# Eleven shifted columns renewed by VectorE alone, and HGRN2's levels on gathered keys and queries, in a two-layer hybrid decoder step

## The chip, the cores and the metric

The kernel runs on one core of one Trainium2 chip. The metric is the device time of one execution, in microseconds (us), taken as the median of several runs. The engines are called as in the profile: PE is TensorE (matrix products), PEld its weight load, DVE is VectorE, ACT is ScalarE, POOL is GpSimd, and SP issues the transfers.

## The reference, cut to what matters

One inference step of a two-layer trunk over a prompt of 256 tokens and 8 samples of 4 tokens each, so 288 token columns, all in fp32. The model has 2048 features.

```python
for l in range(DEPTH):                       # DEPTH = 2
    if l % 2 == 0:                           # retention (4 heads) beside RG-LRU (8 blocks)
        mix = _even_mixer(x, ...)            # x @ w_in (2048 x 6144), ..., @ w_out
    else:                                    # HGRN2: 16 heads, state 128 x 128
        mix = _odd_mixer(x, ...)             # x @ w_in (2048 x 8192), ..., @ w_out
    x = _layer_norm(DN_ALPHA * x + mix, g, b)
    f = _conv_ffn(x, ...)                    # u, v = split(x @ w_up); (gelu(conv(u)) * v) @ w_down
    x = _layer_norm(DN_ALPHA * x + f, g, b)
# HGRN2 (_gla): S_t = diag(f_t) S_{t-1} + k_t v_t^T ;  o_t = S_t^T q_t
# _layer_norm: (x - mean) * rsqrt(var + eps) * g + b
```

All states after the prompt and after the samples are outputs too.

## The kernel before, in words

**Layout.** Features lie on the 128 partitions and the 288 tokens along the free dimension; `x[k]`, k = 0 to 15, is one row of 128 features. Every fp32 operand of a projection is split into a high part in the matrix engine's fp32r format and a low part that is the rest (`xh`, `xl` for x; `wh`, `wl` for weights). A projection is a list of output columns m of 128 features each. `gemm` (L383) computes a group of columns: for each tile (k, m) three products, `wh` with `xh`, `wh` with `xl`, `wl` with `xh`, summed into one PSUM bank of the pool `pm` (four banks). The other four banks are the pool `px`, which the mixers' small products and the sums of the norms use through `psx`. A group of four columns runs k by k over the first 12 rows, then column by column over the last four (`order`, L125).

**Weights.** They come in 1 MB pieces of 16 tiles on SP's queue. ACT copies half a piece (eight tiles) to `wh` (L342), and DVE subtracts to get `wl` (L352), some three halves ahead of use.

**Order.** PE, ACT, DVE and POOL run their instructions in the order in which the program writes them. Side work is written as generators in `Tasks`: `gemm` calls `tasks.tick()` after each tile (three products), a tick counts down all tasks and lets at most one of those that are due take a step, and a task's `yield n` asks for its next step n ticks later.

**Change of stage.** A layer norm needs all of x, but the next projection begins before it is done. Its first columns run on *shifted* operands: x minus a pivot, times the gain, split into `xh` and `xl` (`raw_step`, L571). Two more operand columns hold the gain's and the bias's part, so these products are 290 wide. `close` (L535) sums x and its squares through PE (`lns`, `lnq`, from `laccd` and `laccq`, which POOL adds up) and makes the mean `mu` and `rs`, the reciprocal deviation. `fold` (L648) then puts them into each finished shifted column in PSUM with two DVE operations (L652, L653), after which ACT takes the column out (L405) and its bank is free. Meanwhile `renorm` renews x itself (`ren_step`, L599): it subtracts `mu` (L605, POOL), multiplies by `rs` (L608, POOL and DVE by turns), and applies gain and bias (L612, ACT), one step every REN ticks; and `operands` splits the renewed x into `xh` and `xl` (`op_step`, L626; the low part in L415, POOL and DVE by turns), which may overwrite a row only when the last shifted group has read it (`freed`). `first_groups` (L725) writes this order; `groups_odd_in` and `groups_up` list the groups. There are three such changes: from the even mixer to the first feed-forward part (at 481 us), from there to the odd mixer (at 1325), and from the odd mixer to the second feed-forward part (at 1965). Seven columns are shifted: the output gates of heads 0 to 6, or the v columns of the feed-forward part. They are kept until their head or their u column comes.

**HGRN2's levels.** A head's prompt is treated in two chunks of 128 by doubling block lengths L = 1, 2, ..., 64 (`levels`, L1265). At each level keys of one half of every block meet queries of the other half in one product (`scores`, L1241), and DVE merges the result into the score matrix `AA` under a mask (`keep`, L1250). Then keys and queries are multiplied by the totals of the forget gate, and the totals are joined in pairs (`T`). The product's keys are first copied into one piece, E, by ACT (`gather`, L1235); its queries are read from `qc` in place, with a stride. A level of before stands so in the code:

```python
self.scores(i)                       # product of E and qc
# DVE: k *= totals; sample part of k (L <= 2); T
yield GAP_A                          # 2 ticks
# DVE: qc *= totals; sample part of qc (L <= 2)
self.keep(i)                         # DVE: merge the product into AA
self.gather(i + 1)                   # ACT: E of the next level
yield GAP_B + slow                   # 2 ticks, 3 for heads 0 and 1
```

Heads with three columns (forget f, query q, value v) follow one another every 48 ticks; from head 7 on the head's gate column makes it 64.

**Fourfold copies.** In the retention heads of the even mixer the 32 sample columns of k and v are copied four times side by side on POOL (`v4` in L836, `k4` in L1001), 16 copies of 128x32 per head, so that one transposition (`pst`) spreads them over the partitions.

Of the kernel before, what the change touches and what calls it, by code (L numbers as in the profile page):

```python
# [18 lines left out]
P = 128  # L19
# [28 lines left out]
G0 = 0  # L48
# [7 lines left out]
REN = 4  # L56
LAG = 4
AHEAD = 7
LOG = range(1, 17, 2)
MUG = range(0, 17, 2)  # L60
# [16 lines left out]

def groups_odd_in():
    out = [[48, 49, 50, 51], [52], [53, 54]]
    for h in range(H_HG - 2):  # L80
        out += [[16 + h], [h], [32 + h]] + [[48 + h]] * (h >= AHEAD)
    a, b = H_HG - 2, H_HG - 1
    out += [[16 + a], [a], [16 + b], [b], [32 + a], [48 + a], [32 + b], [48 + b]]
    return [("od_in", list(range(KT)), g) for g in out]
# [6 lines left out]
def groups_up(l, q):  # L91
    ms = [m for f in range(q * FQ, (q + 1) * FQ) for m in (f, FT + f)]
    if q == 0:
        v = ms[1:2 * AHEAD:2]
        out = [v[:4], v[4:5], v[5:]] + [[m] for m in ms[0:2 * AHEAD:2] + ms[2 * AHEAD:]]
    else:
        out = [[m] for m in ms]
    return [(f"up{l}", UP_K[l], g) for g in out]
# [154 lines left out]
def build(tc, A, phases="ACDF"):  # L253
# [11 lines left out]
    with contextlib.ExitStack() as est:  # L265
# [117 lines left out]
        def gemm(mat, ks, ms, rh, rl, need=None, done=None, post=None, w=T):  # L383
            ps = {m: pm.tile([P, 512], F32, tag="pm", name=f"ps_{mat}_{m}_{ks[0]}") for m in ms}
# [29 lines left out]
        def split_lo(k, src, eng=None):  # L414
            (eng or V).tensor_tensor(xl[k], src, xh[k].bitcast(F32), op=ALU.subtract)  # L415
# [36 lines left out]
        class Norm:  # L452
# [82 lines left out]
            def close(self):  # L535
                self.stat(KT - 1)
                yield 9
# [61 lines left out]
            def ren_step(self):  # L599
# [3 lines left out]
                if i < KT:  # L603
                    k = self.order[i]
                    G.tensor_tensor(x[k], x[k], self.mu, op=ALU.subtract)  # L605
                if 0 < i <= KT:
                    k = self.order[i - 1]
                    (G if i in MUG else V).tensor_tensor(x[k], x[k], self.rs, op=ALU.mult)  # L608
# [17 lines left out]
            def op_step(self):  # L626
# [5 lines left out]
                if i > 0:  # L632
                    split_lo(self.order[i - 1], x[self.order[i - 1]], G if i in LOG else V)

            def operands(self):
                while self.no <= KT:
                    if self.op_ready():
                        self.op_step()
                    yield 1
# [85 lines left out]
        def first_groups(mat, prev, gs, done, post=None):  # L725

            gs = iter(gs)
            if isinstance(prev, Norm):
                fold = prev.fold(done)
                gemm(mat, prev.order, next(gs), xhf, xlf, prev.need_raw, fold, w=T + 2)  # L730
                gemm(mat, prev.order, next(gs), xhf, xlf, None, fold, w=T + 2)
                tasks.spawn(prev.operands(), 1)
                gemm(mat, prev.order, next(gs), xhf, xlf, None, fold, prev.freed.add, T + 2)
# [36 lines left out]
        def even_in(eo, ea, o_rg, o_rt, prev, norm):  # L770
# [56 lines left out]
            def vals(h):  # L827
# [4 lines left out]
                def vdone(m, ps):  # L832
                    i = m - 16 - 2 * h
                    S.activation(vt[i], ps[:, :T], AF.Copy)
                    for r in range(4):
                        G.tensor_copy(v44[:, i, r, :], vt[i][:, TP:T])  # L836
# [158 lines left out]
        def ret_inner(rt, h, cv, kk, qq, hd):  # L995
# [3 lines left out]
            for kt in range(2):  # L999
                for r in range(4):  # L1000
                    G.tensor_copy(k44[:, kt, r, :], kk[kt][:, TP:T])  # L1001
# [173 lines left out]
        class HG:  # L1175
# [59 lines left out]
            def gather(self, i):  # L1235

                self.e = self.od.tile([P, P], F32, name=f"E{i}_{self.h}", tag="E", bufs=3)
                cut = lambda a: a.rearrange("p (n c l) -> p n c l", c=2, l=1 << i)
                S.activation(cut(self.e), early_half(self.k, 1 << i), AF.Copy)

            def scores(self, i):  # L1241
# [3 lines left out]
                mm(ps[:, :P], self.e, late_half(self.qc, L, True))  # L1245
# [19 lines left out]
            def levels(self):  # L1265
                h, tl, k, qc = self.h, self.tl, self.k, self.qc
                slow = 1 if h < 2 else 0
# [6 lines left out]
                for i in range(7):  # L1274
                    L = 1 << i
                    self.scores(i)
                    early, late = early_half(k, L), late_half(qc, L, False)
                    V.tensor_tensor(early, early, totals(cur, L, True), op=ALU.mult)
                    W = T if L <= 2 else TP
                    nb = W // (2 * L)  # L1280
                    tv = cur[:, :2 * nb].rearrange("p (n s) -> p n s", s=2)
                    if L <= 2:
# [4 lines left out]
                        V.tensor_tensor(ks, ks, bc(1), op=ALU.mult)  # L1287
                    nt = tl(f"T{i}", (P, nb))
                    V.tensor_tensor(nt, tv[:, :, 0], tv[:, :, 1], op=ALU.mult)
                    yield GAP_A + (G0 if i == 0 else 0)  # L1290
                    V.tensor_tensor(late, late, totals(cur, L, False), op=ALU.mult)
                    if L <= 2:
                        V.tensor_tensor(qs, qs, bc(0), op=ALU.mult)
                    self.keep(i)
# [5 lines left out]
                    yield GAP_B + slow  # L1300
# [321 lines left out]
```

## Time and profile before

| | |
|---|---|
| time, median of three runs | 2830.85 us (2830.67 to 2831.03) |
| profiled execution: time, span | 2834.14 us, 2832.2 us |
| TensorE's mean granted clock | 0.996 of full speed |
| busy share of the span: PE, DVE, ACT, POOL | 98%, 62%, 45%, 20% |
| HBM | 450.71 MB read, 22.19 MB written |
| the chain of work that ended last | PE 88%, DVE 6%, ACT 2%, POOL 2% |

The span is that of one profiled execution and a little shorter than its time, which has what lies around it. Products are pipelined in the matrix engine: one is shown for some 0.3 us, but the next starts 0.13 us after it, so a busy PE is not one at its peak, and the idle time listed before a product is less than what was lost.

### The profile page before, as it was taken

How to read it: one execution, taken by the hardware profiler on the slowest of the kernel's cores; microseconds unless marked ns; L12 is line 12 of the kernel's file. 1: busy time of each engine (PE TensorE's matmuls, PEld its weight loads, DVE VectorE, ACT ScalarE, POOL GpSimd, SP SyncE). 2: the span in 40 equal slices, each digit the busy share in tenths (PEclk: the TensorE clock that was granted, in tenths of full speed). 3: DMA queues.
4: the chain of work that ended last, by engine and by line, in shares of the span. 5: the costliest groups of instructions: out<-in, count | busy, mean ns of one | idle time of the engine just before them, and what ended most of it. 6: DMA issues, size and time to landing. Idle time of an engine off the chain costs nothing.

```text
span 2832.2 us, 51174 instructions
## 1 busy us (share of the span) xinstructions
PE 2786.0 (98%) x21068; PEld 2752.9 (97%) x21068; DVE 1745.1 (62%) x2683; ACT 1277.2 (45%) x2234; POOL 556.7 (20%) x975
## 2 busy tenths in 40 slices
PE   9999999999999999999999999999999999999997
PEld 9999999999999999999999999999999999999997
DVE  7665566854554554558777766676854555554556
ACT  6534445643343443445555545555643443433433
POOL 1411024510000000007332222244400000000016
PEclk9999999999999999999999999999999999999998
DMA  6465444444444445445444444444444444444442
GB/s 250 165 242 201 182 167 167 159 170 164 164 164 165 171 156 177 166 160 182 148 151 161 167 167 155 166 158 162 164 164 172 171 151 177 164 164 168 167 166 90
DMA packets 80153, 476.20 MB, mean 168 GB/s; under 512 B 9392, under 2 KB 17840, under 8 KB 28208
## 3 DMA queue, kind: packets, MB, share of 16 engines
q1 hardware_dynamic: 79920, 472.94, 46.6%
q8 instruction: 165, 2.70, 0.4%
q14 instruction: 68, 0.56, 0.1%
HBM read 450.71 MB, written 22.19 MB: 167 GB/s over the span
## 4 chain that ended last, share of the span: by engine, by line
PE 88%; DVE 6%; ACT 2%; POOL 2%; issue 1%; DMA 0%; SPq 0%; DVEq 0%; ACTq 0%; POOLq 0%
PE ps_up L279 36%; PE ps_dn L279 18%; PE ps_od_in L279 12%; PE ps_ev_in L279 9%; PE ps_ev_out L279 4%; PE ps_od_out L279 4%; DVE wl L352 2%; PE hl L279 1%; DVE xl L580 1%; ACT wh L342 1%; PE hpo L279 1%; DVE xl L415 1%; DVE x L608 1%; PE po L279 0%; PE hpS L279 0%
## 5 line engine op out<-in xcount | busy, mean ns | idle before, releaser
L352 DVE TENSOR_TENSOR wl<-wr,wh 128x1024 fp32r<-128x1024 f32 (+1 forms) x818 | 1024.4, 1258 | 145.8 <-ACT wh L342 71.5
L342 ACT ACTIVATE wh<-wr 128x1024 fp32r<-128x1024 f32 (+1 forms) x818 | 845.5, 1049 | 352.8 <-PE ps_dn L279 294.1
L279 PE MATMUL ps_up<-xl,wh 128*128 128x288 f32 (+1 forms) x2816 | 832.8, 296 | 2.7 <-DVE xl L415 2.1
L279 PE MATMUL ps_up<-xh,wh 128*128 128x288 f32 (+1 forms) x2816 | 831.6, 295 | 3.2 <-ACT vs L405 3.2
L279 PE MATMUL ps_up<-xh,wl 128*128 128x288 f32 (+1 forms) x2816 | 831.7, 295 | 0.0
L279 PEld LDWEIGHTS ps_up<-xh,wh 128*128 128x128 f32 x2816 | 530.4, 188 | 3.8 <-ACT vs L405 3.7
L279 PEld LDWEIGHTS ps_up<-xl,wh 128*128 128x128 f32 x2816 | 529.5, 188 | 4.2 <-DVE xl L415 3.1
L279 PEld LDWEIGHTS ps_up<-xh,wl 128*128 128x128 f32 x2816 | 530.8, 188 | 0.0
L279 PE MATMUL ps_dn<-hh,wh 128*128 128x288 f32 x1408 | 417.4, 296 | 0.0
L279 PE MATMUL ps_dn<-hl,wh 128*128 128x288 f32 x1408 | 416.7, 296 | 0.0
L279 PE MATMUL ps_dn<-hh,wl 128*128 128x288 f32 x1408 | 415.1, 295 | 0.0
L279 PE MATMUL ps_od_in<-xh,wh 128*128 128x288 f32 (+1 forms) x1024 | 320.1, 313 | 0.1
L279 PE MATMUL ps_od_in<-xl,wh 128*128 128x288 f32 (+1 forms) x1024 | 302.8, 296 | 2.8 <-DVE xl L415 2.8
L279 PE MATMUL ps_od_in<-xh,wl 128*128 128x288 f32 (+1 forms) x1024 | 302.3, 295 | 0.0
L1415 POOL COPY fco<-us 128x2 f32<-128x2 f32 x88 | 18.4, 209 | 1367.3 <-ACT us L403 1367.3
L279 PEld LDWEIGHTS ps_dn<-hl,wh 128*128 128x128 f32 x1408 | 265.7, 189 | 0.1
L279 PEld LDWEIGHTS ps_dn<-hh,wl 128*128 128x128 f32 x1408 | 265.8, 189 | 0.0
L279 PEld LDWEIGHTS ps_dn<-hh,wh 128*128 128x128 f32 x1408 | 265.1, 188 | 0.1
L279 PE MATMUL ps_ev_in<-xh,wh 128*128 128x288 f32 x768 | 234.2, 305 | 0.3 <-ACT wh L342 0.3
L279 PE MATMUL ps_ev_in<-xh,wl 128*128 128x288 f32 x768 | 228.3, 297 | 0.5 <-DVE wl L352 0.5
L279 PE MATMUL ps_ev_in<-xl,wh 128*128 128x288 f32 x768 | 228.3, 297 | 0.0
L279 PEld LDWEIGHTS ps_od_in<-xl,wh 128*128 128x128 f32 x1024 | 193.6, 189 | 5.0 <-DVE xl L415 3.7
(316 smaller groups left out, 3913.7 us busy)
## 6 DMA issues: line engine op xcount, KB each, us to landing
wr<-w SPq DMA_DIRECT2D x404, 1024.0 KB, 4.8
s<-sret SPq DMA_DIRECT2D x16, 512.0 KB, 6.0
rs<-s SPq DMA_DIRECT2D x16, 512.0 KB, 4.7
hs<-shg SPq DMA_DIRECT2D x16, 512.0 KB, 5.6
gs<-hs SPq DMA_DIRECT2D x16, 512.0 KB, 2.6
wr<-w SPq DMA_DIRECT2D x6, 512.0 KB, 5.9
x<-x SPq DMA_DIRECT2D x16, 144.0 KB, 5.1
y<-x SPq DMA_DIRECT2D x16, 144.0 KB, 1.8
```

The source lines that it names most:

```text
L279: return nc.tensor.matmul(o, l, r, start=start, stop=stop, skip_group_check=True)
L342: S.activation(hi[:, d], src, AF.Copy)
L352: V.tensor_tensor(lo[:, d], src, hi[:, d].bitcast(F32), op=ALU.subtract)
L415: (eng or V).tensor_tensor(xl[k], src, xh[k].bitcast(F32), op=ALU.subtract)
L580: V.scalar_tensor_tensor(xl[k], x[k], self.col("lng", k), xh[k].bitcast(F32), ALU.mult, ALU.subtract)
L608: (G if i in MUG else V).tensor_tensor(x[k], x[k], self.rs, op=ALU.mult)
L1415: G.tensor_copy(fc4[:, f, 0, :], s[:, TP:TP + 2])
```

## The change

- The number of shifted columns goes from 7 to 11. They run as four together, three singly, and four together; the last four take their PSUM banks from `px`. Each feed-forward part then has eleven v columns first and its eleven u columns of the first quarter behind them.
- Renewing x (subtraction and multiplication) and the low parts of the renewed operands are all made by DVE; POOL has none of them. `renorm` steps every 6 ticks instead of 4, `operands` every 2 instead of 1. `close` waits 14 ticks instead of 9 before its sums.
- The levels of HGRN2 gather the queries too (L, beside E, four buffers of each), multiply keys and queries one behind the other, gather for the next level at once, and write the product of level i two ticks after that and its merge another two ticks later. Level 1 (L = 2), whose product also reads sample columns in place, keeps its product at the start. The extra tick for heads 0 and 1 goes.
- The fourfold copies are one instruction with a broadcast source instead of four.

```diff
@@ -45,7 +45,6 @@
 D0 = 8
-G0 = 0
 GAP_A = 2
@@ -53,11 +52,9 @@
 WARM = 8
-REN = 4
+REN = 6
 LAG = 4
-AHEAD = 7
-LOG = range(1, 17, 2)
-MUG = range(0, 17, 2)
+AHEAD = 11
@@ -75,8 +72,13 @@
+def ahead(ms):
+
+    return [ms[:4]] + [[m] for m in ms[4:-4]] + [ms[-4:]]
+
+
 def groups_odd_in():
-    out = [[48, 49, 50, 51], [52], [53, 54]]
+    out = ahead([48 + h for h in range(AHEAD)])
     for h in range(H_HG - 2):
@@ -92,7 +94,7 @@
         v = ms[1:2 * AHEAD:2]
-        out = [v[:4], v[4:5], v[5:]] + [[m] for m in ms[0:2 * AHEAD:2] + ms[2 * AHEAD:]]
+        out = ahead(v) + [[m] for m in ms[0:2 * AHEAD:2] + ms[2 * AHEAD:]]
     else:
@@ -380,8 +382,8 @@
-        def gemm(mat, ks, ms, rh, rl, need=None, done=None, post=None, w=T):
-            ps = {m: pm.tile([P, 512], F32, tag="pm", name=f"ps_{mat}_{m}_{ks[0]}") for m in ms}
+        def gemm(mat, ks, ms, rh, rl, need=None, done=None, post=None, w=T, bank=(pm, "pm")):
+            ps = {m: bank[0].tile([P, 512], F32, tag=bank[1], name=f"ps_{mat}_{m}_{ks[0]}") for m in ms}
             for k, m in order(ks, ms):
@@ -411,8 +413,8 @@
-        def split_lo(k, src, eng=None):
-            (eng or V).tensor_tensor(xl[k], src, xh[k].bitcast(F32), op=ALU.subtract)
+        def split_lo(k, src):
+            V.tensor_tensor(xl[k], src, xh[k].bitcast(F32), op=ALU.subtract)
@@ -534,7 +536,7 @@
                 self.stat(KT - 1)
-                yield 9
+                yield 14
                 ps_s = psx(f"lns_{self.idx}")
@@ -602,10 +604,10 @@
                     k = self.order[i]
-                    G.tensor_tensor(x[k], x[k], self.mu, op=ALU.subtract)
+                    V.tensor_tensor(x[k], x[k], self.mu, op=ALU.subtract)
                 if 0 < i <= KT:
                     k = self.order[i - 1]
-                    (G if i in MUG else V).tensor_tensor(x[k], x[k], self.rs, op=ALU.mult)
+                    V.tensor_tensor(x[k], x[k], self.rs, op=ALU.mult)
                 if 1 < i:
@@ -630,13 +632,13 @@
                 if i > 0:
-                    split_lo(self.order[i - 1], x[self.order[i - 1]], G if i in LOG else V)
+                    split_lo(self.order[i - 1], x[self.order[i - 1]])
...
                         self.op_step()
-                    yield 1
+                    yield 2
@@ -728,9 +730,10 @@
                 gemm(mat, prev.order, next(gs), xhf, xlf, prev.need_raw, fold, w=T + 2)
-                gemm(mat, prev.order, next(gs), xhf, xlf, None, fold, w=T + 2)
+                for _ in range(AHEAD - 8):
+                    gemm(mat, prev.order, next(gs), xhf, xlf, None, fold, w=T + 2)
                 tasks.spawn(prev.operands(), 1)
-                gemm(mat, prev.order, next(gs), xhf, xlf, None, fold, prev.freed.add, T + 2)
+                gemm(mat, prev.order, next(gs), xhf, xlf, None, fold, prev.freed.add, T + 2, (px, "px"))
                 prev.raw_done = True
@@ -832,8 +835,7 @@
                     S.activation(vt[i], ps[:, :T], AF.Copy)
-                    for r in range(4):
-                        G.tensor_copy(v44[:, i, r, :], vt[i][:, TP:T])
+                    G.tensor_copy(v44[:, i], vt[i][:, TP:T].unsqueeze(1).to_broadcast([P, 4, TS]))
@@ -997,8 +999,7 @@
             for kt in range(2):
-                for r in range(4):
-                    G.tensor_copy(k44[:, kt, r, :], kk[kt][:, TP:T])
+                G.tensor_copy(k44[:, kt], kk[kt][:, TP:T].unsqueeze(1).to_broadcast([P, 4, TS]))
             hd["k4"] = k4
@@ -1234,15 +1235,18 @@
-                self.e = self.od.tile([P, P], F32, name=f"E{i}_{self.h}", tag="E", bufs=3)
-                cut = lambda a: a.rearrange("p (n c l) -> p n c l", c=2, l=1 << i)
-                S.activation(cut(self.e), early_half(self.k, 1 << i), AF.Copy)
+                L = 1 << i
+                self.e[i], self.l[i] = [self.od.tile([P, P], F32, name=f"{n}{i}_{self.h}", tag=n, bufs=4) for n in "EL"]
+                cut = lambda a: a.rearrange("p (n c l) -> p n c l", c=2, l=L)
+                S.activation(cut(self.e[i]), early_half(self.k, L), AF.Copy)
+                cut = lambda a: a.rearrange("p (c n l) -> p c n l", c=2, l=L)
+                S.activation(cut(self.l[i]), late_half(self.qc, L, True), AF.Copy)
...
                 self.ps = ps = psx(f"hl{self.h}_{i}")
-                mm(ps[:, :P], self.e, late_half(self.qc, L, True))
+                mm(ps[:, :P], self.e.pop(i), self.l.pop(i))
                 if L == 2:
@@ -1264,7 +1268,7 @@
                 h, tl, k, qc = self.h, self.tl, self.k, self.qc
-                slow = 1 if h < 2 else 0
+                self.e, self.l = {}, {}
                 self.AA = tl("AA", (P, TP))
@@ -1273,9 +1277,11 @@
                     L = 1 << i
-                    self.scores(i)
+                    if L == 2:
+                        self.scores(i)
                     early, late = early_half(k, L), late_half(qc, L, False)
                     V.tensor_tensor(early, early, totals(cur, L, True), op=ALU.mult)
+                    V.tensor_tensor(late, late, totals(cur, L, False), op=ALU.mult)
                     W = T if L <= 2 else TP
@@ -1285,19 +1291,19 @@
                         V.tensor_tensor(ks, ks, bc(1), op=ALU.mult)
+                        V.tensor_tensor(qs, qs, bc(0), op=ALU.mult)
                     nt = tl(f"T{i}", (P, nb))
                     V.tensor_tensor(nt, tv[:, :, 0], tv[:, :, 1], op=ALU.mult)
-                    yield GAP_A + (G0 if i == 0 else 0)
-                    V.tensor_tensor(late, late, totals(cur, L, False), op=ALU.mult)
-                    if L <= 2:
-                        V.tensor_tensor(qs, qs, bc(0), op=ALU.mult)
-                    self.keep(i)
                     if L == 2:
...
                         self.gather(i + 1)
-                    yield GAP_B + slow
+                    yield GAP_A
+                    if L != 2:
+                        self.scores(i)
+                    yield GAP_B
+                    self.keep(i)
                 self.tot = cur
...
```

## Rows read from the trace of the kernel before

**Rows 1.** The page: busy time and share of the span by engine.
```profile
PE 2786.0 (98%) x21068; PEld 2752.9 (97%) x21068; DVE 1745.1 (62%) x2683; ACT 1277.2 (45%) x2234; POOL 556.7 (20%) x975
```

**Rows 2.** Stretches: length, then busy (xinstructions) PE PEld DVE ACT POOL, clock, DMA, GB/s.
```profile
122.00:128.00 6.00, 6.00 (x53) 4.89 (x52) 3.46 (x5) 2.48 (x6) 0.00 (x0) 0.72 0.55 188
...
481.00:508.00 27.00, 26.79 (x196) 26.35 (x196) 27.00 (x28) 18.74 (x31) 20.55 (x18) 1.00 0.33 119
...
560.00:600.00 40.00, 40.00 (x304) 40.00 (x303) 27.48 (x39) 20.29 (x41) 11.96 (x48) 1.00 0.48 173
```

**Rows 3.** Whom TensorE waited for: us in total, times, longest.
```profile
PE hl L279 <- DVE q L1293: 4.3, 9, 0.6
...
PE hl L279 <- DVE q L1291: 3.6, 7, 1.5
...
PE ps_up L279 <- ACT vs L405: 3.2, 2, 1.6
...
PE ps_od_in L279 <- DVE xl L415: 2.8, 3, 1.7
...
PE hl L279 <- ACT E L1239: 2.6, 5, 0.8
...
PE ps_up L279 <- DVE xl L415: 2.1, 3, 0.9
...
PE lnq L279 <- POOL laccq L482: 1.4, 1, 1.4
```

**Rows 4.** Timeline of PE: start, us, instruction, idle time before it and its releaser.
```profile
121.04 0.33 PE L282 MATMUL pst<-ident,k 128*128 128x128 f32 x1 [2.14 <-POOL k L1001]
...
1656.09 0.29 PE L279 MATMUL ps_od_in<-xh,wl 128*128 128x288 f32 x1
...
1656.91 0.46 PE L279 MATMUL hl<-q,E 128*128 128x128 f32 x2 [0.53 <-DVE q L1293]
...
1658.80 0.38 PE L279 MATMUL hl<-q,E 128*128 128x128 f32 x2
```

**Rows 5.** DVE's groups by line, 481 to 538 us, change of stage.
```profile
L352 DVE TENSOR_TENSOR wl<-wr,wh 128x1024 fp32r<-128x1024 f32 x16 | 23.7, 1481 | 0.0
...
L608 DVE TENSOR_TENSOR x<-x,lpiv 128x288 f32<-128x288 f32 x8 | 7.2, 906 | 0.0
...
L415 DVE TENSOR_TENSOR xl<-x,xh 128x288 fp32r<-128x288 f32 x8 | 6.0, 775 | 1.5 <-ACT xh L412 1.5
...
L652 DVE SCALAR_TENSOR_TENSOR ps_up<-laccp,lw,ps_up 128x288 f32<-128x288 f32 x7 | 3.6, 513 | 1.2 <-ACT lw L651 1.2
...
L553 DVE RECIPROCAL lpiv<-lpiv 128x288 f32<-128x288 f32 x1 | 1.9, 1940 | 0.0
```

**Rows 6.** DVE's groups by line, 560 to 620 us, middle of a projection.
```profile
L352 DVE TENSOR_TENSOR wl<-wr,wh 128x1024 fp32r<-128x1024 f32 x20 | 24.4, 1221 | 3.1 <-PE ps_up L279 1.8 <-ACT wh L342 1.3
...
L1421 DVE SCALAR_TENSOR_TENSOR uy<-us,par,uy 128x304 f32<-128x304 f32 x12 | 6.4, 535 | 0.4
...
L1439 DVE TENSOR_TENSOR hl<-ug,hh 128x288 fp32r<-128x288 f32 x7 | 3.2, 455 | 1.7 <-ACT hh L1437 1.7
```

**Rows 7.** Timeline of POOL: first multiplication of the renewing after the stage changes.
```profile
492.93 0.87 POOL L608 TENSOR_TENSOR x<-x,lpiv 128x288 f32<-128x288 f32 x1 [3.46 <-DVE lpiv L553]
```

**Rows 8.** Timeline of DVE inside a head's levels.
```profile
1655.26 1.21 DVE L352 TENSOR_TENSOR wl<-wr,wh 128x1024 fp32r<-128x1024 f32 x1
...
1656.39 0.38 DVE L1291 TENSOR_TENSOR q<-q,T 128x128 f32<-128x128 f32 x1
```

**Rows 9.** ACT's groups by line, 1640 to 1772 us, four heads.
```profile
L1239 ACT ACTIVATE E<-k 128x128 f32<-128x128 f32 x28 | 8.8, 316 | 31.5 <-DVE k L1278 26.5 <-DVE T L1289 5.0
```

**Rows 10.** Timeline of POOL ahead of the state products of retention head 0.
```profile
109.86 3.23 POOL L836 COPY v<-vt 128x32 f32<-128x32 f32 x4
...
120.35 1.22 POOL L1001 COPY k<-k 128x32 f32<-128x32 f32 x8
```

**Rows 11.** Groups by line, whole span: one piece of 128x128 on POOL.
```profile
L1220 POOL COPY hv<-v 128x128 f32<-128x128 f32 x16 | 6.7, 417 | 83.1 <-ACT v L403 83.1
```

## The prediction

> **What bounds the kernel now.** The page comes first: TensorE is busy for 98% of the span, DVE for 62%, ACT for 45% [rows 1]. So the only time to be won is time in which TensorE starts nothing, or runs at a lower clock. The table of stretches gives the rate to compare with: undisturbed, it starts 304 matmuls in 40.00 us, 0.1316 us each [rows 2]. One column of a projection has 16 x 3 = 48 matmuls, 6.32 us; a tick (three matmuls) is 0.395 us. The list of TensorE's waits then tells where it falls behind [rows 3]. A wait costs more than its idle time, as the timeline shows: a product due 0.13 us after its predecessor at 1656.09 starts at 1656.91, 0.69 us late, for 0.53 us of listed idle time, and its pair lasts 0.46 us instead of the undisturbed 0.38 of 1658.80 [rows 4]. So I add 0.16 + 0.08 = 0.24 us to each listed wait. Grouped by what the change touches:
>
> - The level products `hl` of HGRN2 wait 4.3 + 3.6 + 2.6 = 10.5 us in 21 waits: 10.5 + 21 x 0.24 = 15.5 us.
> - The three changes of stage (shifted columns and what follows them) wait 3.2 + 2.8 + 2.1 + 1.4 = 9.5 us in 9 waits: 11.7 us.
> - `pst` in the even mixer waits 2.1 us for the copies of k on POOL [rows 4], 2.3 with the supplement. In 122 to 128 us behind it the granted clock is 0.72: part of the stretch went at 1.2 instead of 2.4 GHz, 6 x 0.28 = 1.7 us more [rows 2]. Together 4.0 us.
>
> That is 31.2 us, about the most that this change can free.
>
> **Part 1: eleven shifted columns, DVE alone.** At the change of stage at 481 us DVE is busy for 27.00 of 27.00 us [rows 2]. The reason is in its durations: the split of a weight tile takes 1.48 us there, the renewing multiplication 0.91, the renewed low half 0.78 [rows 5]; where POOL does little, the split takes 1.22 us and the nearest two-input operation on 128x288 takes 0.455 us [rows 6]. What differs is POOL, which works on the same renewing. The Trainium skill, "SBUF — State Buffer", Who interferes with whom, says that a DVE operation with two SBUF inputs and a POOL operation that reads SBUF shut each other out; by that rule the low prices return when POOL leaves, which is the sum below; without it the 48 moved and remaining operations would stay at 0.84 us and the sum would be 88.8 us. The trace so far agrees with it (1.48 against 1.22 us). By the rows alone the moved operations lie between 0.455 and 0.91 us.
>
> I take 0.46 us, the row without POOL. Over 11 x 6.32 = 69.5 us per stage DVE then has: 22 weight splits x 1.22 = 26.8; 32 renewing operations x 0.46 = 14.7; 16 renewed low halves x 0.46 = 7.4; 16 raw low halves x 0.535 (the nearest three-operand row) = 8.6; 11 folds of two operations x 0.51 = 11.2; the reciprocal 1.9. Sum 70.6 us in 69.5. DVE is full, not overfull: it may lag by 1 to 2 us, and that is to be held against the slacks of the new order.
>
> - The fifth column waited for the PSUM bank of the first, whose release was queued behind DVE's inflated work (3.2 us in two stages). The first column ends at step 52 of 64, so release has 12 x 0.395 = 4.7 us; with a lag of 2 us, the fold's 1.0 and about as much on ACT it fits. The last four columns take banks of the other pool and wait for nobody.
> - Behind the shifted columns the first ordinary column waited for renewed low halves (2.8 + 2.1 us). Now the last four columns go k by k, so operand rows come free every 4 x 0.395 = 1.6 us instead of 0.8, and renewing has 69.5 instead of 44.2 us: begun some 14 us into the stage (12 now [rows 7], 2 later by the longer `close`), 18 steps x 6 ticks x 0.395 = 43 us end at 57. The last four rows come free only at the end, but are wanted 12 steps, 4.7 us, later.
> - `close` yields 14 ticks instead of 9, 2.0 us, which covers the 1.4 us of `lnq` waiting for POOL. Mean and deviation come 2.0 us later; the first fold, at step 52 or 20.5 us, wants them 6 us after that.
> - Twelve more columns, 576 matmuls, are 290 instead of 288 wide: no row tells the two apart; by two columns of 288 each would take 0.1316 x 2/288 = 0.001 us more, 0.5 us in all. Eleven values and then eleven u columns reorder the feed-forward part; its DVE is idle for 31% there [rows 2] and the down projection wants the last operand 31 steps later: nothing, or one late chain of 1 us at each.
>
> Of 11.7 us I leave 2.2 for lags: **-9.5 us** (bounds -11.7 and -3), and **+0.5**.
>
> **Part 2: the levels.** Before, a level multiplies q two ticks (0.8 us) ahead of the product that reads it, and copies k into E at the same time. At 1656.91 the 0.38 us multiplication of q had stood behind a 1.21 us weight split [rows 8]; that alone makes the wait. After, both multiplications stand together, ACT copies both into E and L at once, and the product comes six ticks (2.4 us) after the copies are issued, for levels 0 and 1 four (1.6 us). The chain is 2 x 0.38 on DVE and 2 x 0.32 on ACT [rows 8, 9], 1.4 us: a lag of 1.0 us is covered where 0.4 was; at level 1, with the sample columns in the chain, next to none. DVE's work is the same, only moved, and its multiplication of q no longer waits for the product ahead of it, which reads L. ACT gets 112 more copies of 0.316 us, 35 us; at 45% busy it has room for them [rows 1], but they stand in its queue waiting for two DVE operations instead of one, ahead of weight splits that have three tiles of lead.
>
> Eleven gates come first now, so heads 7 to 10 have three columns instead of four to hide in. I leave a fifth of 15.5 us standing: **-12.4 us** (bounds -15.5, and -3 if ACT takes DVE's place).
>
> **Part 3: copies in one piece.** `pst` starts at 121.04 us after 2.1 us of waiting, so it was due at 118.9; POOL reaches the copies of k only at 120.35 us [rows 4, 10]. Ahead of them the four copies of v take 3.23 us beside DVE [rows 10]. One copy of 128x128 takes 0.42 us [rows 11]: the first v group shrinks by up to 2.8 us, and half of k is there 0.42 us after its start instead of four small copies later. The start moves to about 118 and `pst` finds its data. The idle time that cost the clock goes with it: **-4.0 us** (bounds -4.0 and -1, where the single copy is stretched as the four were and the clock falls again).
>
> **Sum.** -9.5 + 0.5 - 12.4 - 4.0 = -25.4 us. The profiled execution took 2834.14 us (span 2832.2, 1.9 around it), 3.3 above the median of 2830.85. So 2808.7 for a profiled one, and a median of **2805.4 us**.
>
> **Rivals.** *DVE becomes the bound (slower).* [...] By rows: if the 48 renewing and low-half operations of a stage cost 0.65 us, half way between 0.455 and the mean of 0.91 and 0.78, DVE needs 48 x 0.19 = 9.1 us more, 79.7 in 69.5, and TensorE waits for it in each of three stages: 3 x 10.2 = 31, less parts 2 and 3 (16.4), +14 us: 2845. It decides from 16.4 / 3 = 5.5 us beyond the columns, 0.55 us an operation. For it speaks the full row of DVE; against it, that 0.455 was measured on an engine busy for 69%.
> *ACT becomes the late engine of the levels.* Part 2 then gives 3 us: 2815. For it speaks that ACT already stands idle for 31.5 us in four heads, waiting for DVE ahead of E [rows 9], and a copy that waits holds up what is behind it; against it, that the scores now come three times as late.
> *Nothing moves.* The waits only change their names: 2831. Against it, they have three separate causes.
>
> **Chances.** The forecast 0.66 (own range 2798 to 2811); ACT late 0.18 (2811 to 2821); no change 0.07; DVE the bound 0.09. The range takes in the first two: 2797 to 2821. A measurement tells 0.2%, 5.7 us, from nothing. Faster 0.84, same 0.07, slower 0.09.
>
> **What would show it.** Right: DVE's weight split near 1.22 us and the moved operations near 0.46 in the first 70 us of each stage; no wait of TensorE for `vs` and `lnq`, under 1 us for `xl`; `hl` waits under 3 us; `pst` without wait and the clock 1.00 behind it; 224 copies into E and L on ACT. Wrong: TensorE waiting for `wl` in the shifted columns, or `hl` waiting for L on ACT as long as it did for q.

## The result, and the profile after

The changed kernel takes 2807.12 us (median of 4 runs, 2805.96 to 2808.47) against 2830.94 before: a ratio of 0.9914, 95% interval 0.9898 to 0.9930, so 0.7 to 1.0% faster. The forecast was 2805.4, the range 2797 to 2821. The profiled execution took 2807.34 us, its span 2805.6.

The page's busy times, to be set beside [rows 1], show why so little moves: TensorE was and stays the bound, and only its idle time could be won. POOL lost 126 us, ACT gained 34, DVE as a whole 4.5.

```profile
PE 2776.2 (99%) x21068; PEld 2750.9 (98%) x21068; DVE 1749.6 (62%) x2803; ACT 1311.2 (47%) x2366; POOL 430.2 (15%) x831
```

Then the list of TensorE's waits, for [rows 3]. The three lines of `hl` there are replaced by one, `L`, with 4.8 us in place of 10.5; `vs`, `xl` and `lnq` are gone; the wait for POOL's `k` fell from 2.1 to 1.1 us.

```profile
PE hl L281 <- ACT L L1243: 4.8, 6, 0.9
PE pst L284 <- POOL k L1002: 1.1, 1, 1.1
```

The stretches of [rows 2], and one more that spans the first 70 us of the stage with eleven shifted columns. Columns as there: busy time of PE, PEld, DVE, ACT and POOL, then the clock.

```profile
122.00:128.00 6.00, 6.00 (x63) 4.91 (x63) 4.38 (x8) 3.53 (x6) 0.00 (x0) 1.00 0.58 229
481.00:508.00 27.00, 27.00 (x200) 26.79 (x199) 24.25 (x41) 20.65 (x38) 2.34 (x4) 1.00 0.44 157
560.00:600.00 40.00, 40.00 (x304) 40.00 (x304) 28.84 (x45) 20.87 (x46) 11.05 (x49) 1.00 0.49 180
479.00:549.00 70.00, 70.00 (x519) 69.79 (x518) 57.88 (x98) 47.62 (x84) 3.03 (x4) 1.00 0.46 166
```

At 481 us DVE is no longer full, though it does all of the renewing: 24.25 of 27 us for 41 instructions, where 28 had filled it. DVE's groups by line, 481 to 538 us, say how, against [rows 5]: the weight split fell from 1481 to 1214 ns, the renewing multiplication from 906 to 451, the renewed low half from 775 to 455.

```profile
L354 DVE TENSOR_TENSOR wl<-wr,wh 128x1024 fp32r<-128x1024 f32 x19 | 23.1, 1214 | 0.0
L610 DVE TENSOR_TENSOR x<-x,lpiv 128x288 f32<-128x288 f32 x16 | 7.2, 451 | 0.0
L607 DVE TENSOR_TENSOR x<-x,laccp 128x288 f32<-128x288 f32 x16 | 7.2, 450 | 0.0
L582 DVE SCALAR_TENSOR_TENSOR xl<-x,par,xh 128x288 fp32r<-128x288 f32 x12 | 6.7, 601 | 0.0
...
L417 DVE TENSOR_TENSOR xl<-x,xh 128x288 fp32r<-128x288 f32 x7 | 3.2, 455 | 1.4 <-ACT xh L414 1.4
```

Where the time came from is seen by the length of each stage, from its first matmul to the first of the next, taken from the timeline of TensorE in both traces:

| stage | before us | after us | difference |
| --- | --- | --- | --- |
| even mixer, in-projection | 374.20 | 371.97 | -2.23 |
| first up projection of the even layer | 145.63 | 142.07 | -3.57 |
| odd mixer, in-projection and heads | 531.57 | 514.01 | -17.56 |
| first up projection of the odd layer | 145.45 | 141.88 | -3.57 |
| each of the other stages | | | within 0.03 |

With 0.27 us for a later start that makes 26.6 us between the two profiled spans; the medians differ by 23.8. The profiled run of before was 3.3 us above its median; which stage held these 3 us is not known. Between profiled runs with the same code in a stage its length agrees within 0.15 us, except in the even mixer's in-projection: it took 370.24 to 371.97 us in the nine profiled runs that have the changed kernel's code there. So the -2.23 is the least certain row of the table.

One wait is left over and is to be read closely. The timeline of all engines around the longest one (matmuls and weight loads between left out):

```profile
1488.48 1.90 POOL L1387 TENSOR_TENSOR hs<-hs,T 128x1024 f32<-128x1024 f32 x1
...
1488.54 2.09 DVE L1283 TENSOR_TENSOR k<-k,f 128x128 f32<-128x128 f32 x1 [0.36 <-ACT E L1241]
...
1490.04 0.30 PE L281 MATMUL ps_od_in<-xh,wl 128*128 128x288 f32 x1
1490.48 0.38 DVE L1284 TENSOR_TENSOR q<-q,f 128x128 f32<-128x128 f32 x1
1490.66 0.32 ACT L1241 ACTIVATE E<-k 128x128 f32<-128x128 f32 x1 [1.95 <-DVE k L1283]
...
1490.89 0.32 ACT L1243 ACTIVATE L<-q 128x128 f32<-128x128 f32 x1
...
1491.27 0.49 PE L281 MATMUL hl<-L,E 128*128 128x128 f32 x2 [0.93 <-ACT L L1243]
```

The list blames ACT, but ACT had been idle for 1.95 us. DVE's multiplication of k takes 2.09 us instead of 0.40: it starts 0.06 us after POOL's multiplication of the state and ends just after it. From 1490.04 to 1491.27 is 1.23 us, against 0.13 undisturbed. This happens in five heads, always in level 1's product, the one with four ticks.

### The profile page after: what moved, and what is told of

The parts are those of the page before. It is cut to its first block, busy times and chain, and to the rows that moved or that the text cites. A ratio compares the mean times of both kernels' runs of the same rounds, so it can differ in the third digit from the quotient of the medians.

```text
span 2805.6 us, 51262 instructions
## 1 busy us (share of the span) xinstructions
PE 2776.2 (99%) x21068; PEld 2750.9 (98%) x21068; DVE 1749.6 (62%) x2803; ACT 1311.2 (47%) x2366; POOL 430.2 (15%) x831
## 4 chain that ended last, share of the span: by engine, by line
PE 97%; DVE 1%; ACT 1%; DMA 0%; issue 0%; POOL 0%; SPq 0%; DVEq 0%
PE ps_up L281 40%; PE ps_dn L281 20%; PE ps_od_in L281 14%; PE ps_ev_in L281 11%; PE ps_ev_out L281 4%; PE ps_od_out L281 4%; PE hl L281 1%; PE hpo L281 1%; PE po L281 0%; DVE k L1283 0%; PE hpS L281 0%; PE hpc L281 0%; DVE x L695 0%; PE pc L281 0%; PE hpn L281 0%; PE pn L281 0%
## 5 line engine op out<-in xcount | busy, mean ns | idle before, releaser
L354 DVE TENSOR_TENSOR wl<-wr,wh 128x1024 fp32r<-128x1024 f32 (+1 forms) x818 | 1008.1, 1238 | 126.1 <-ACT wh L344 60.1
L405 ACT ACTIVATE us<-ps_up 128x256 f32<-128x256 f32 (+1 forms) x176 | 41.7, 290 | 339.2 <-PE ps_up L281 339.2
```

What stands on the lines that cost most here:

```text
L354: V.tensor_tensor(lo[:, d], src, hi[:, d].bitcast(F32), op=ALU.subtract)
L405: S.activation(o, ps[:, c], func)
```

## The experiments

All are edits of the changed kernel; "before" took 2831.05 to 2831.33 us beside them.

**Part 2 undone** (`undo_levels`). The levels as before: one copy E, the product first, q multiplied two ticks ahead of it.

```diff
-                S.activation(cut(self.l[i]), late_half(self.qc, L, True), AF.Copy)
...
-                mm(ps[:, :P], self.e.pop(i), self.l.pop(i))
+                mm(ps[:, :P], self.e, late_half(self.qc, L, True))
...
-                    if L == 2:
-                        self.scores(i)
+                    self.scores(i)
...
-                    V.tensor_tensor(late, late, totals(cur, L, False), op=ALU.mult)
...
+                    V.tensor_tensor(late, late, totals(cur, L, False), op=ALU.mult)
```

> The changed kernel with HGRN2's levels as they were before (queries read in place, one copy a level); eleven shifted columns on DVE alone and the copies in one piece stay. Theory (the levels' product came too soon after the operations it reads): the waits of TensorE for q and E return, about 10 us of listed idle time in some 20 waits, and the time is about 12 us above the changed kernel, 2819. Rival (the saving in the odd mixer comes from the shifted columns, whose stage change lies there too): no more than 4 us above it, 2811.

2817.76 us (0.9952, 0.9938 to 0.9967), 10.6 above the changed kernel; the odd mixer's stage 525.35 us, 11.34 longer. TensorE's waits have the old names again:

```profile
PE hl L282 <- DVE q L1295: 5.8, 12, 0.6
PE hl L282 <- ACT E L1241: 2.9, 5, 1.3
PE hl L282 <- DVE q L1293: 1.5, 6, 0.3
```

Part 2 is worth 10.6 us by the medians and 11.3 by its stage, about what was expected.

**Which half of part 2** (`early_product`). Both operands still gathered, but the product comes first at every level, four ticks after the copies.

```diff
-                    if L == 2:
-                        self.scores(i)
+                    self.scores(i)
...
-                    yield GAP_A
-                    if L != 2:
-                        self.scores(i)
-                    yield GAP_B
+                    yield GAP_A + GAP_B
```

> The changed kernel with every level's product at the start of its level, four ticks (1.6 us) after its copies are issued instead of six; only level 1 stood so. Copies and multiplications stay where they are. Theory (what counts is the slack between the copies and the product): waits for L on ACT at several levels of a head, 4 to 10 us more than the changed kernel, 2811 to 2817. Rival (what counts is that DVE no longer waits for the product before it multiplies q): no difference, 2807.

2819.71 us (0.9960, 0.9945 to 0.9975), the stage 527.28 us. It loses more than all of part 2, and more than the 4 to 10 us expected: the copies are worth something only because they let the product come later; alone they put ACT's second copy into the chain.

```profile
PE hl L281 <- ACT L L1243: 10.6, 20, 1.0
```

**Part 3 undone** (`undo_copies`).

```diff
-                    G.tensor_copy(v44[:, i], vt[i][:, TP:T].unsqueeze(1).to_broadcast([P, 4, TS]))
+                    for r in range(4):
+                        G.tensor_copy(v44[:, i, r, :], vt[i][:, TP:T])
```

(and the same for k)

> The changed kernel with four copies in place of each broadcast copy in the even mixer. Theory: the wait of the state products for k returns to 2.1 us, the granted clock falls behind it (0.72 in the 6 us after), and the even mixer takes 2 to 3 us more: 2809.5. Rival (POOL was late because of what else stands in its queue, so the copies' number does not matter): the wait stays at 1.1 us and the time at 2807.

2809.68 us (0.9923, 0.9908 to 0.9938), 2.6 above; but its four runs (2807.55 to 2810.97) overlap with those of the changed kernel (2805.96 to 2808.47). The wait for k is 2.2 us again, and the stretch behind it at 122 to 128 us has the clock of [rows 2] again, 0.72 (PE 5.16 busy, since the wait lies in it here):

```profile
122.00:128.00 6.00, 5.16 (x33) 4.35 (x37) 4.44 (x7) 2.37 (x5) 1.22 (x9) 0.72 0.58 190
```

The wait's 1.1 us more and the clock's 6 x 0.28 = 1.7 us make 2.8, close to the 2.6. The length of this run's stage, 375.62 us, says less: in 14 to 20 us, long before the copies, its clock was granted at 0.72 too, where the changed kernel has 1.00.

**The small casts moved** (`cols_later`). In the changed kernel the first copy of v takes 0.28 us, yet POOL reaches k at 120.57 us, no sooner than in [rows 10]. The timeline of POOL says what it does between:

```profile
110.73 0.28 POOL L838 COPY v<-vt 128x128 f32<-128x128 f32 x1
110.96 0.69 POOL L565 CAST xh<-gbh 128x2 fp32r<-128x2 f32 x1
111.60 1.24 POOL L566 CAST xl<-gbl 128x2 fp32r<-128x2 f32 x1
112.78 1.19 POOL L565 CAST xh<-gbh 128x2 fp32r<-128x2 f32 x1
113.92 1.19 POOL L566 CAST xl<-gbl 128x2 fp32r<-128x2 f32 x1
...
117.36 0.18 POOL L565 CAST xh<-gbh 128x2 fp32r<-128x2 f32 x1
...
120.45 0.18 POOL L566 CAST xl<-gbl 128x2 fp32r<-128x2 f32 x1
120.57 0.52 POOL L1002 COPY k<-k 128x128 f32<-128x128 f32 x2
```

Four casts of two elements a row, 0.18 us each in a quiet stretch, now stand where the copy of v stood, beside DVE's weight splits at 111.60 to 115.06, and take 4.31 us. Thirteen pairs more stand ahead of k. The edit spawns them behind the first values:

```diff
+            tasks.spawn(norm.cols(prev), 60)
...
-            if ph != phases[-1]:
+            if ph not in ("A", phases[-1]):
```

> The changed kernel with the even mixer's small copies of the gain's and bias's columns issued later, behind the first retention head's fourfold copies on POOL instead of ahead of them. Theory (what remains of the wait for k, 1.1 us, is the queue of some 32 small casts ahead of the copies): the wait goes, 1.3 us less than the changed kernel, 2805.8. Rival (the copies come late because of the scans and gates before): the wait stays.

2805.65 us (0.9910, 0.9895 to 0.9925), 1.5 less; `pst` is not in the list of waits any more. The gain alone is not clear of noise: the runs overlap with the changed kernel's, and the stage's 370.34 us instead of 371.97 lies within what it varies by. `seven_cols` below repeats the step with runs that do not overlap. The bad place is not gone either: four copies of 128x1 and 128x8 (`rgh`) stand in it now and take 0.70 to 1.25 us each. What let POOL reach k at 115.68 us are the thirteen pairs that no longer stand ahead of it.

**The longer `close`** (`close_nine`): `yield 14` back to `yield 9`.

> The changed kernel with the wait of 9 ticks instead of 14 before the norm's sums. Theory: at the change to the odd mixer TensorE waits again for POOL's sum of squares, 1.4 us idle, 1.6 in all; the other changes of stage stay without wait: 2808.7. Rival (mean and deviation 2 us earlier are worth as much): no difference or a gain, 2806.

2808.78 us (0.9923, 0.9906 to 0.9939), 1.7 above the changed kernel, with runs that overlap; the odd mixer's stage is 1.74 us longer, clear of what it varies by, with the old wait of [rows 3] back:

```profile
PE lnq L281 <- POOL laccq L484: 1.4, 1, 1.4
```

**DVE alone, but seven columns** (`seven_dve`). The groups and spacing of before; POOL stays out, and `close` keeps its 14 ticks and the last two columns the banks of `px`.

```diff
-REN = 6
+REN = 4
...
-AHEAD = 11
+AHEAD = 7
...
-    return [ms[:4]] + [[m] for m in ms[4:-4]] + [ms[-4:]]
+    return [ms[:4], ms[4:5], ms[5:]]
...
-                    yield 2
+                    yield 1
...
-                for _ in range(AHEAD - 8):
+                for _ in range(1):
```

> Seven shifted columns again, with the groups and the steps of renewing as before (every 4 and 1 ticks), but all renewing on DVE, and the last two columns in the other PSUM pool. Theory (POOL's presence made DVE slow, and the longer time is needed because DVE does it all): no wait for the release of the first bank, DVE's weight split at 1.22 us, but waits for the renewed low halves at the end of the shifted columns, 2 to 4 us a stage, so 2 to 8 us above the changed kernel. Rival (the columns do not matter, POOL's absence does it all): no wait at any change of stage, time as the changed kernel, 2807.

2801.15 us (0.9894, 0.9879 to 0.9908): not slower but 6.0 us faster. The waits that were expected for the renewed low halves did not come: no wait is listed at any change of stage, and none for `hl`. DVE is busy for 43.26 of the 44 us that seven columns give, and nothing waits for it:

```profile
479.00:523.00 44.00, 44.00 (x325) 43.79 (x325) 43.26 (x80) 36.23 (x67) 3.04 (x4) 1.00 0.42 145
```

The up stages are 0.43 and 0.39 us shorter than with eleven columns (192 matmuls fewer of 290 columns, about 2 ns each), the odd mixer's 4.75.

**Eleven columns, POOL sharing as before** (`eleven_pool`).

```diff
-                    V.tensor_tensor(x[k], x[k], self.mu, op=ALU.subtract)
+                    G.tensor_tensor(x[k], x[k], self.mu, op=ALU.subtract)
...
-                    V.tensor_tensor(x[k], x[k], self.rs, op=ALU.mult)
+                    (G if i in MUG else V).tensor_tensor(x[k], x[k], self.rs, op=ALU.mult)
...
-                    split_lo(self.order[i - 1], x[self.order[i - 1]])
+                    split_lo(self.order[i - 1], x[self.order[i - 1]], G if i in LOG else V)
```

> Eleven shifted columns, with renewing shared between POOL and DVE as before, all else as changed. Theory (POOL slows DVE): weight splits near 1.45 us and renewing near 0.9 us on DVE, the waits for the release of the first bank return in the two changes into the feed-forward parts, 1.6 us each; none for the renewed low halves, which have 25 us more: 3 to 5 us above the changed kernel, 2811. Rival (the longer time alone cures the stage changes): no waits, 2807.

2806.65 us (0.9913, 0.9897 to 0.9930): not 3 to 5 us above but the same as the changed kernel, with no wait at a change of stage, though DVE's prices are the dear ones (by line, 479 to 523 us):

```profile
L356 DVE TENSOR_TENSOR wl<-wr,wh 128x1024 fp32r<-128x1024 f32 x14 | 20.2, 1451 | 0.0
L584 DVE SCALAR_TENSOR_TENSOR xl<-x,par,xh 128x288 fp32r<-128x288 f32 x13 | 10.1, 820 | 0.0
L612 DVE TENSOR_TENSOR x<-x,lpiv 128x288 f32<-128x288 f32 x7 | 5.2, 750 | 0.0
```

**The same with a renewing step every four ticks** (`eleven_ren4`): `REN = 6` to `REN = 4`.

> Eleven shifted columns with POOL sharing the renewing as before the change, and a renewing step every four ticks as before instead of every six. Theory: the spacing of the steps cured the wait of the fifth column (vs), since DVE at its dear prices (weight split 1.42, two-input operations 0.79 us) cannot do a step in 4 x 0.395 = 1.6 us beside the weight splits; then 1 to 1.6 us of vs waits return in each of two or three stages and the time is 2809 to 2812. Rival: the number of columns alone cured it; then no wait at any change of stage, 2806.7 +/- 1 as with the wide spacing.

2806.71 us (0.9917, 0.9900 to 0.9933); no such wait. My theory of the spacing falls: DVE is busy for 43.24 of 44 us, and nothing waits for it.

```profile
479.00:523.00 44.00, 44.00 (x325) 43.79 (x324) 43.24 (x50) 34.29 (x60) 31.01 (x26) 1.00 0.41 144
```

Nor can the number of columns have cured the wait of the fifth: up to it this run and the kernel before write the same groups and the same steps into the feed-forward part. What differs there is `close`, 14 ticks instead of 9. The fold of the first column, whose bank the fifth one needs, and the wait, in the kernel before:

```profile
508.91 0.51 DVE L652 SCALAR_TENSOR_TENSOR ps_up<-laccp,lw,ps_up 128x288 f32<-128x288 f32 x1
...
510.57 0.40 PE L279 MATMUL ps_up<-xh,wh 128*128 128x290 f32 x1 [1.63 <-ACT vs L405]
```

and the fold in this run:

```profile
503.64 0.51 DVE L656 SCALAR_TENSOR_TENSOR ps_up<-laccp,lw,ps_up 128x288 f32<-128x288 f32 x1
```

Counted from the start of the stage (481.48 and 478.94 us), the fold starts at 27.43 us before and at 24.70 here, and the renewing on POOL at 5.17 and 6.96: with the later `close`, three renewing multiplications instead of four stand ahead of the fold on DVE. So the traces point to `close` as the cure of this wait where POOL shares the work. That is read from two traces; no run has POOL's share with 9 ticks and eleven columns.

**POOL kept busy beside DVE** (`pool_busy`). DVE renews alone, eleven columns, but POOL adds two useless sums of 128x288 at each step, 32 in a stage.

```diff
                     V.tensor_tensor(x[k], x[k], self.mu, op=ALU.subtract)
+                    for _ in range(2):
+                        G.tensor_tensor(self.accd, self.accd, self.accq, op=ALU.add)
```

> The changed kernel with useless work for POOL while DVE renews: two additions of 128x288 on the used-up sums at each of the 16 steps, none of which DVE or any product waits for. Theory (the two engines shut each other out, and that was what slowed DVE): DVE's renewing rises from 0.45 to 0.8 us or more and its weight splits from 1.21 to 1.4, DVE is full again, and waits at the stage changes return: 3 to 30 us more than the changed kernel. Rival (DVE was slow before for its own load only): operations stay at 0.45, time as the changed kernel, 2807.

2827.03 us (10 runs; 0.9986, 0.9977 to 0.9996), 20 above the changed kernel: nearly all of its gain is gone. DVE's prices rise although its work is the same, and TensorE waits for the fold of the first column (groups by line, then the list of waits):

```profile
L354 DVE TENSOR_TENSOR wl<-wr,wh 128x1024 fp32r<-128x1024 f32 x10 | 15.7, 1566 | 0.0
L582 DVE SCALAR_TENSOR_TENSOR xl<-x,par,xh 128x288 fp32r<-128x288 f32 x12 | 9.7, 846 | 0.0
L607 DVE TENSOR_TENSOR x<-x,laccp 128x288 f32<-128x288 f32 x8 | 7.8, 970 | 0.0
```

```profile
PE ps_up L281 <- ACT lw L655: 11.0, 2, 5.5
...
PE ps_od_in L281 <- ACT lw L655: 2.4, 1, 2.4
```

Not all of the 20 us are waits: behind the two long ones the granted clock is 0.72 (510 to 516 us) and 0.62 (1981 to 1990 us), 1.7 and 3.4 us more. In `eleven_pool` the prices on DVE were nearly as dear and nothing waited; here DVE has all of the renewing to do at them.

**POOL's state multiplication four ticks later** (`state_later`), to test the collision at 1488.5 us.

```diff
+                yield 4
                 sb = s0.rearrange("p (b d) -> p b d", b=NB)
```

> The changed kernel with POOL's multiplication of the state (hs by T, 1.9 us) issued four ticks later, behind level 0's product. Theory: the five waits of 0.93 us for L at level 1 (1.1 us of delay each, start to start 1.22 instead of 0.13 us) come from DVE's first multiplication of k of a head taking 2.09 instead of 0.40 us because it starts beside that POOL operation; moved, the waits go from 4.8 us to under 2 and the time falls by 4 to 6 us, to about 2802. Rival one: ACT is simply late at level 1, whose product has only four ticks; then the waits stay at 4 to 5 us and the time at 2807 +/- 1. Rival two: the POOL operation only meets the next multiplication instead, at level 1 or 2; the waits change their places, and the time is within 2 us of 2807.

2806.53 us (0.9914, 0.9900 to 0.9929): no gain that can be told from none, where 4 to 6 us were expected; the second rival is what came. That the multiplication is long because of POOL is shown all the same. The first multiplication of k takes 0.41 us in each of the five heads that had 2.09, and level 1's product no longer waits. But POOL now meets the multiplication two levels on (timeline, other rows left out), and level 3's product waits 0.51 us:

```profile
1492.12 1.90 POOL L1388 TENSOR_TENSOR hs<-hs,T 128x1024 f32<-128x1024 f32 x1
1492.28 1.89 DVE L1283 TENSOR_TENSOR k<-k,T 128x128 f32<-128x128 f32 x1
...
1494.50 0.31 ACT L1243 ACTIVATE L<-q 128x128 f32<-128x128 f32 x1
...
1494.86 0.38 PE L281 MATMUL hl<-L,E 128*128 128x128 f32 x1 [0.51 <-ACT L L1243]
```

Listed waits for L fall from 4.8 to 2.5 us, the stage by only 0.56; where the rest of the difference went was not read.

**The best of them** (`seven_cols`: `seven_dve` and `cols_later` together).

> Seven shifted columns with DVE alone (2801.15 so far), and the 13 pairs of small casts on POOL moved behind the first values of the even mixer, so that the copies of k no longer stand behind them (-1.5 us on the changed kernel). Theory: the two savings lie in different stages and add: 2799.5 +/- 0.7. Rival: they don't add, 2801 +/- 0.5.

2799.46 us (2799.30 to 2799.64; 0.9889, 0.9875 to 0.9904): the savings add, and it beats both kernels, the changed one by 7.7 us. No wait is left that the change was about (the whole list of TensorE's waits):

```profile
PE warm L281 <- DVE ones_d L1479: 1.1, 1, 1.1
PE ps_ev_in L281 <- ACT wh L344: 1.0, 1, 1.0
PE pga L281 <- issue: 0.5, 1, 0.5
PE pa L281 <- DVE q L820: 0.4, 1, 0.4
```

**And the later state multiplication on top** (`seven_all`).

> The same with seven columns, and POOL's multiplication of the state issued four ticks later too. Theory: with seven columns no product of the levels waits for L any more, so the move has nothing to win: 2799.5 +/- 0.7, as without it. Rival: the collision still costs something at seven columns (two multiplications of k still took 1.2 us): 2798 or less. Second rival: POOL's later multiplication meets something else, 2801 or more.

2799.38 us (0.9889, 0.9875 to 0.9904), the same: with seven columns there was nothing left to win there. One wait for L came back (0.6 us in the list), without a price that the time would show.

## Why the prediction came out right, and where it did not

The time, 1.7 us from the forecast, is right, and so is the case (three separate waits removed). The parts are less exact than their sum, which is partly luck.

**Part 1: forecast -9.5 + 0.5, by stages -13.4.** The two up stages gave 3.57 each; of the odd mixer's 17.56, 11.34 are part 2's, which leaves 6.2. That is beyond the bound of -11.7. By the medians parts 2 and 3 leave 23.8 - 10.6 - 2.6 = 10.6 for it, which is within the bound; most of the difference is the 3 us by which the profiled run of before lay above its median. The supplement of 0.24 us a wait holds: the first up stage had four listed waits of 2.9 us, so 3.9 with it, and it became 3.57 shorter while it paid 0.43 for wider columns. What was mis-sized is the 2.2 us kept back for lags, which did not come, and two short waits for `xl` (L580, 0.5 us) that were not counted. The odd mixer's listed waits make 5.2 with the supplement; why it gave 6.2 is open.

The durations were right (1.22 forecast, 1.214 measured; 0.46 and 0.450 to 0.455), but for the raw low halves, 0.60 instead of 0.535. The Trainium skill, "SBUF — State Buffer", Who interferes with whom, which stood behind them, agrees with `pool_busy`: useless work on POOL alone brings back 1.566 and 0.970 us. Two steps failed:

- *"DVE is full, not overfull", 70.6 us of work in 69.5.* It was busy for 57.9 of 70 us. The durations of the 98 instructions there, added up by line, make 64.0 us; some of the 16 renewed low halves and the last folds come after the 70 us. The other 6 us are overlap: on DVE's timeline a subtraction of 0.45 us is followed after 0.37 us, a weight split of 1.21 after 1.14. Here the sum of durations overprices a busy DVE by about a tenth. The 2.2 us that I kept back for lags weren't needed.

```profile
495.91 0.45 DVE L607 TENSOR_TENSOR x<-x,laccp 128x288 f32<-128x288 f32 x1
496.28 0.44 DVE L610 TENSOR_TENSOR x<-x,lpiv 128x288 f32<-128x288 f32 x1
496.65 1.21 DVE L354 TENSOR_TENSOR wl<-wr,wh 128x1024 fp32r<-128x1024 f32 x1
497.79 0.45 DVE L607 TENSOR_TENSOR x<-x,laccp 128x288 f32<-128x288 f32 x1
```

- *That the waits go because the time is longer and POOL is out of the way.* Not both are needed: `seven_dve` has the old 44 us and no wait; `eleven_pool` and `eleven_ren4` have the old prices and no wait. But all three keep the later `close` and the banks of `px`, which I had counted for `lnq` and the last columns only. For the fifth column the cure under the old prices is neither the columns nor the spacing, and by the traces it is `close` (see `eleven_ren4`); with DVE alone 9 ticks were enough for it too (`close_nine` has no such wait). Seven columns with POOL's share, the later `close` and `px` were not run, and part 1 as a whole was not undone, so how much of it the columns are worth is open. The same runs overturn what I held of seven columns before `seven_dve` ran.

One cost was undersized. The four more wide columns cost 0.43 and 0.39 us in the two up stages, where I had put 0.5 for all three stages; and the step *"heads 7 to 10 have three columns instead of four to hide in"* is where eleven columns are really paid. With seven columns none of the five long waits for L occurs, and the odd mixer's stage is 4.75 us shorter. The heads then meet POOL's state multiplication at other moments; long k multiplications still occur, of 1.22 us in two heads and of 1.28, 1.86 and 1.96 in three others, without a listed wait. That the head's length sets which instruction POOL meets is argued from these traces, and `state_later` shows that shifting it by four ticks changes the place.

**Part 2: forecast -12.4, measured -11.3 by stages (10.6 by medians).** The mechanism is right: `early_product` shows that the gain is the slack between copies and product, and that the copies matter only because they let the product come later. The 3 us left standing were laid to ACT's two copies in a row and to fewer columns; measured are 4.8 us listed, and their cause is POOL beside DVE. The collision was in the trace of before too: 2.10 us for a k multiplication at 1559.04, beside POOL's at 1558.98. I took 0.38 us as DVE's price in the levels without looking at the longest ones. "Under 3 us" was wrong, and "waiting for L on ACT as long as it did for q" did not come true; 224 copies are there, 112 into each tile, and ACT at 47% bears them.

**Part 3: forecast -4.0, measured -2.2 by the stage, 2.6 by undoing it, both rough.** The clock came back (1.00 against 0.72), and k's two copies take 0.52 us instead of 1.22. The step that failed is *"the first v group shrinks by up to 2.8 us"*, carried on to the start of k: the copy did shrink from 3.23 to 0.28, but the four casts behind it in POOL's queue took its place beside the same weight splits and grew to 4.31 us, so that k starts at 120.57 instead of 120.35 and half of the wait stays. `cols_later` removes that half.

**The rivals.** DVE as the bound did not come; `pool_busy` shows it with POOL at work beside all of the renewing: 20 us, the clock's 5 among them, at 0.97 us an operation. ACT as the late engine came in name alone. The sum was right by luck: part 1, undersized by 4.4 us by stages (1.6 by medians), made up for parts 2 and 3, oversized by 1.1 and 1.8 (1.8 and 1.4 by medians).

## What to carry to other kernels

Before an operation is taken off a shared queue, read what stands behind it: the next one may inherit its bad place, as the casts did. Work handed to a second engine to relieve a full one can raise the price of everything on the first; here DVE alone did the whole renewing in the 44 us in which the two together had been late (with the earlier `close`). And take the longest of a group as well as its mean: a wait put down to the last engine of a chain had its cause two engines earlier.

## What the runs showed of the hardware

- A DVE multiplication of 128x128 with two operands that starts during POOL's of 128x1024 ends just after it: it takes 2.09 us instead of 0.40 when it starts 0.06 us behind one of 1.90 us, 1.89 when it starts 0.16 us behind (`state_later`), and 1.22 when it starts 0.93 us behind (`seven_dve`, 1538.44 us).
- Casts of 128x2 on POOL, 0.18 us each in a quiet stretch, take 1.19 to 1.24 us beside DVE's weight splits.
- Operations on DVE follow each other sooner than they end: 0.37 us from start to start at a duration of 0.45, as shown above.
- An idle time of 1.1 us ahead of `pst` left the clock behind it at 1.00, that is 2.4 GHz; after 2.1 and 2.2 us it was granted at 0.72, a mean of that level and 1.2 GHz over 122 to 128 us. The length of one wait alone does not tell it: in `undo_copies` the clock is 0.72 in 14 to 20 us too, behind listed waits of at most 0.8 us, and in `eleven_pool` it stays at 1.00 there behind waits of at most 0.9.
